# Block sums of a 7-product down projection: made on GpSimd in earlier stages and passed through DRAM, instead of inside the projection

## The chip, the cores and the metric

One core of one Trainium2 chip. The metric is the device time of one execution in microseconds, as the median of several runs.

## The reference, cut to what matters

One decoder layer on x of 1024 rows and 1024 columns, all in float32:

```python
p = rms_norm(x, norm_mix) @ w_in              # one projection into three groups of heads
y = concat(conv_mixer(p), nsa_mixer(p), rwkv7(p))
x = x + y @ w_out                             # out-projection, residual
h = rms_norm(x, norm_ffn)
g = causal_dwconv(h @ w_gate, width 3)        # 2816 channels
x = x + (silu(g) * (h @ w_up)) @ w_down       # w_down is 2816 x 1024
return rms_norm(x, norm_final)
```

The change concerns the last product, A @ W with A = silu(g) * (h @ w_up).

## The kernel before, in words

A tile framework puts the instructions of the whole program in an order for each engine ahead of time; every engine then runs its own list strictly in that order, and waits where an operand is not there. Every DMA is issued by SP, which also works through its list in order and waits there for the data that a store needs or for the buffer that a load fills. Float32 products are made of three TensorE matmuls: `split` (L118 to L121) lets ACT round an operand to a high part and DVE subtract it to get the low part, and `mm3` (L226 to L229) adds high x high, low x high and high x low.

The stages, by the time of the profiled execution:

- To about 400 us: norm, in-projection, convolution and most of the RWKV part. The RWKV part has two halves of channels and two of the sequence; for each there is a solve (`V`, L513 to L534: a chain of dependent small operations on GpSimd, each L528 product followed by an L530 sum) and then a chain of matmuls on TensorE (`C`, first the 32x32 matmuls of L550, which read the tile `DF`). The solve V10 and the solve V11, and the chains C10 and C11, run beside the attention, with high priority. The solve writes its result to DRAM; `DF` is loaded from there (L543).
- 400 to about 717 us: the attention, eight query tiles `attn_tile` (L821 to L933) in the order 7, 6, 5, 4, 0, 3, 2, 1. Of each tile, two operations are made on GpSimd (L849, L857: the sums of the compressed scores, whose result goes to the transposes L862 on TensorE) and most of the softmax on DVE (L911 scales the probabilities `pp`). The tile's result goes to DRAM as `md` (L933). SP loads a tile's queries `QS` (L831, L832) when the buffer of two tiles earlier is free.
- To about 850 us: the out-projection (`out_tile`, L959 on) reads `md` back, splits it (`mix`), multiplies with w_out, and adds the residual; then the second norm and the operands of h for the gate and up products.
- 850 to 1264 us: `ffn_up`. For each of 22 blocks of 128 channels it makes gate and up of all 1024 rows with 7 products instead of 8 (Winograd's form of Strassen's scheme on 2x2 blocks), 84 matmuls per block. GpSimd makes four sums `S` of the block's weights per product group (L1050), about one block ahead. DVE makes the block of A in two tiles `prod` of 128 channels by 512 rows (L1079), which are stored to DRAM (`pd`).
- 1264 to 1531 us: `ffn_down`, the same scheme on A @ W: A is cut into 2x2 blocks (two halves of channels, 11 blocks of 128 each, by two halves of rows), W into 2x2 blocks (two halves of channels by two halves of columns). Seven runs, each one product of 11 f-steps x 4 row tiles x 3 matmuls, 924 matmuls of 128x512 in all. Run 1 needs A11 and B11 as they are; the others need the sums S1 to S4 of blocks of A and T1 to T4 of blocks of W. The helpers g1 to g3 (L1123 to L1169) load 55 blocks of A and 55 of W of 256 KB and make these sums in place, per f-step, in the run that needs them first: T3 and T4 on DVE, the other six on GpSimd, 88 in all (all recorded as L1124). Each run then splits both operands (tiles `sp`). Besides, GpSimd adds the residual (L1202, 16 times) and multiplies by the norm's weight (8 times).

Of the kernel before, what the change touches and what calls it, by code (L numbers as in the profile page):

```python
# [19 lines left out]
class K:  # L20
    def __init__(self, tc, a, out, ctx, bufs=None):
        self.tc, self.nc, self.a, self.out, self.ctx = tc, tc.nc, a, out, ctx
        self.B = dict(b2=20, wraw=2, whi=2, wlo=2, t4=4, rraw=2, cy=2, hx=12, ev=3, cv=2, lora=2, rb=20, at=2, pr=7, rt=2,
                      QS=2, pp=6, q8=2, pT=5, xn=8, h2=14, graw=2, prod=4, ft=4, u=4, wr2=4, wfh=3, wfl=3, S=2, p1=2, om=6, grow=2, pre=2, ap=(), wf=("own", "wf", "om"), hd=("vector",) * 4, tq=((0, 1, 2, 3),), ttag=("tr", "rw"),
# [999 lines left out]
    def ffn_up(self, H):  # L1024
        nc, a = self.nc, self.a
        v, s, gp = nc.vector, nc.scalar, nc.gpsimd
        self.pd = [[self.dram.tile([P, 512], F32, name=f"pd{ft}{h}") for h in range(2)] for ft in range(22)]
        for ft in range(22):
# [7 lines left out]
            def prod(bank, raw, part, first=False):  # L1036
                w = self.B["wf"][(self.nw if ft >= self.B["pre"] else self.nw % 2) % len(self.B["wf"])]
# [64 lines left out]
            out(0, u2)  # L1102

    def ffn_down(self):
# [9 lines left out]
        def A(t, m, k, f):

            nc.sync.dma_start(t, self.pd[k * F + f][1 - m])
            return t

        def Bw(t, k, n, f):
            nc.sync.dma_start(t, W[(k * F + f) * P:(k * F + f) * P + P, n * 512:n * 512 + 512])  # L1120
            return t

        def e(key, x, y, z, op=ALU.subtract):  # L1123
            getattr(nc, self.B["de"][key]).tensor_tensor(x, y, z, op=op)  # L1124
            return x
        a11, a21, b11, b12, b22 = ([None] * F for _ in range(5))
# [4 lines left out]
        def g1(f):  # L1131
            a11[f] = A(self.b2() if f < 10 else x4("r4"), 0, 0, f)
            b11[f] = Bw(self.b2() if f < 10 else x4("r4"), 0, 0, f)
            return a11[f], b11[f]
# [8 lines left out]
        def g2(f):  # L1143
            e("T1", b11[f], b12[f], b11[f])
            e("T2", b12[f], b22[f], b11[f])
            return A(x4("ta"), 0, 1, f), Bw(x4("tb"), 1, 0, f)

        def g4(f):
            t = Bw(x4("tb"), 1, 0, f)
            e("T4", t, t, b12[f])  # L1150
            a22 = A(x4("ta"), 1, 1, f)
            e("S1", a21[f], a21[f], a22, ALU.add)
            e("S2", a11[f], a22, a11[f])
            return a22, t

        def g6(f):
            return a11[f], b12[f]

        def g6b(f):
            e("S4", a11[f], A(x4("ta"), 0, 1, f), a11[f])  # L1160

        def g5(f):
            return a21[f], b11[f]

        def g3(f):
            return a11[f], b22[f]
# [236 lines left out]
```

## Time and profile before

| | us |
|---|---|
| three runs | 1527.68, 1532.06, 1541.17; median 1532.06 |
| the profiled execution | 1533.06, of which the span that the trace shows is 1531.3 |
| TensorE busy | 1431.6 (93%) |
| TensorE's weight loads | 1135.8 (74%) |
| VectorE (DVE) | 1042.6 (68%) |
| ScalarE (ACT) | 684.2 (45%) |
| GpSimd (POOL) | 488.6 (32%) |

The span is cut below into the stages named above. A row of a stage gives the busy time of each engine in it, the share of full speed at which TensorE's clock was granted, and the share of time and the rate at which DMAs moved data.

### The profile page before, as it was taken

To read this page: it belongs to the slowest core of one execution; us is meant where nothing else is said; L and a number is where in the kernel's file an instruction comes from. 1 tells how busy PE (TensorE), PEld (TensorE's weight loads), DVE (VectorE), ACT (ScalarE), POOL (GpSimd) and SP (SyncE) were. 2 spreads that over 40 slices of the span, in tenths; PEclk is the share of its full clock that TensorE was granted. 3 is DMA by queue.
4 is the path that set the end of the run, shared out by engine and by line. 5 is a ranking of instruction groups with operands and counts; after the bars stand their busy time and mean duration, and the time that the engine had idled before them with its cause. 6 is when DMAs were issued, how large, how long until landed. Compare 5 with 4: busy or idle time off the path is not lost.

```text
span 1531.3 us, 22605 instructions
## 1 busy us (share of the span) xinstructions
PE 1431.6 (93%) x8025; PEld 1135.8 (74%) x8025; DVE 1042.6 (68%) x2193; ACT 684.2 (45%) x1361; POOL 488.6 (32%) x585
## 2 busy tenths in 40 slices
PE   6999679999799999998899999999999999897897
PEld 5887457777677777775687788888888887685686
DVE  6247695453586778587267767767767668979976
ACT  6432354534266567677133534334433333343453
POOL 1004887910420050001001223323323315849820
PEclk9999787989799999999999999999999999998999
DMA  6142223433710112114522122222222229163302
GB/s 188 37 120 56 52 83 87 144 93 108 193 32 15 32 39 64 55 39 129 179 90 76 55 69 83 89 77 83 77 89 83 67 93 375 43 203 121 117 1 110
DMA packets 182916, 143.41 MB, mean 94 GB/s; under 512 B 53715, under 2 KB 143124, under 8 KB 182804
## 3 DMA queue, kind: packets, MB, share of 16 engines
q1 hardware_dynamic: 182804, 141.98, 30.5%
q8 instruction: 63, 1.03, 0.3%
q14 instruction: 49, 0.40, 0.1%
HBM read 103.92 MB, written 38.01 MB: 93 GB/s over the span
## 4 chain that ended last, share of the span: by engine, by line
PE 75%; DVE 11%; DMA 5%; POOL 3%; issue 2%; ACT 1%; SPq 1%; DVEq 0%; POOLq 0%; ACTq 0%
PE mm L229 13%; PE gb L229 12%; PE ga L229 9%; PE rw L229 8%; PE gc L229 8%; PE tr L918 5%; PE av L926 4%; DVE sp L121 4%; PE tr L229 3%; PE mm L893 2%; PE mm L894 2%; POOL sT L530 1%; POOL sx L528 1%; PE pm L493 1%; DVE cacc L272 1%
## 5 line engine op out<-in xcount | busy, mean ns | idle before, releaser
L229 PE MATMUL mm<-hT,whi 128*128 128x512 f32 x608 | 204.8, 418 | 0.0
L229 PE MATMUL mm<-hT,wlo 128*128 128x512 f32 x304 | 127.8, 422 | 20.3 <-DVE wlo L121 20.3
L229 PEld LDWEIGHTS mm<-hT,whi 128*128 128x128 f32 x608 | 120.2, 200 | 29.4 <-issue 1.6
L1050 POOL TENSOR_TENSOR S<-wraw,wr 128x512 f32<-128x512 f32 x22 | 28.5, 1297 | 257.9 <-DVE or L107 96.1
L921 ACT ACTIVATE pT<-tr 128x512 f32<-128x512 f32 (+1 forms) x152 | 80.0, 537 | 62.6 <-PE tr L918 61.3
L926 PE MATMUL av<-pT,V 128*64 128x128 f32 x1056 | 95.2, 286 | 4.0 <-ACT pT L921 3.9
L279 POOL TENSOR_TENSOR cacc<-cacc,ctap 128x512 f32<-128x512 f32 x60 | 91.1, 1542 | 17.7 <-ACT ctap L278 17.5
L229 PE MATMUL rw<-sp,sp 128*128 128x512 f32 x330 | 90.0, 397 | 7.1 <-DVE sp L121 6.6
L918 PE MATMUL tr<-idn,pp 128*128 128x128 f32 x528 | 89.6, 288 | 0.1
L229 PEld LDWEIGHTS mm<-hT,wlo 128*128 128x128 f32 x304 | 60.8, 200 | 38.6 <-DVE wlo L121 21.4
L229 PE MATMUL tr<-sp,sp 128*128 128x512 f32 x330 | 88.4, 395 | 0.0
L229 PE MATMUL rw<-woh,mix 128*128 128x512 f32 x240 | 78.9, 405 | 6.4 <-DVE xn L976 5.2
L926 PEld LDWEIGHTS av<-pT,V 128*64 128x64 f32 x1056 | 59.2, 136 | 28.9 <-issue 11.0
L229 PEld LDWEIGHTS rw<-sp,sp 128*128 128x128 f32 x330 | 62.6, 191 | 22.6 <-DVE sp L121 8.8
L893 PE MATMUL mm<-KH,QS 128*128 128x512 f32 (+2 forms) x192 | 74.1, 394 | 4.0 <-DMA QS<-qd 2.5
L918 PEld LDWEIGHTS tr<-idn,pp 128*128 128x128 f32 x528 | 55.7, 141 | 28.6 <-issue 27.3
L121 DVE TENSOR_TENSOR sp<-b,sp 128x512 fp32r<-128x512 f32 x60 | 65.5, 1104 | 13.4 <-ACT sp L120 13.3
L229 PEld LDWEIGHTS tr<-sp,sp 128*128 128x128 f32 x330 | 63.1, 191 | 13.4
L849 POOL TENSOR_TENSOR cmp<-cmp,cmx 128x512 f32<-128x512 f32 (+7 forms) x8 | 5.4, 680 | 206.2 <-DVE cmx L847 137.0
L120 ACT ACTIVATE whi<-wraw 128x512 fp32r<-128x512 f32 x55 | 34.6, 628 | 78.7 <-PE mm L229 60.3
L121 DVE TENSOR_TENSOR wlo<-wraw,whi 128x512 fp32r<-128x512 f32 x55 | 42.3, 771 | 34.9 <-ACT whi L120 34.8
L528 POOL TENSOR_TENSOR sx<-sN,sT 128x60 f32<-128x60 f32 (+24 forms) x124 | 43.8, 353 | 65.4 <-DMA sN<-dn 57.0
(460 smaller groups left out, 3846.3 us busy)
## 6 DMA issues: line engine op xcount, KB each, us to landing
wr<-in_ffn_w_gate_dram SPq DMA_DIRECT2D x44, 256.0 KB
wraw<-in_ffn_w_up_dram SPq DMA_DIRECT2D x44, 256.0 KB
pd<-prod SPq DMA_DIRECT2D x44, 256.0 KB
ta<-pd SPq DMA_DIRECT2D x33, 256.0 KB
wraw<-in_w_in_dram SPq DMA_DIRECT2D x30, 256.0 KB
tb<-in_ffn_w_down_dram SPq DMA_DIRECT2D x22, 256.0 KB
rb<-in_ffn_w_down_dram SPq DMA_DIRECT2D x20, 256.0 KB
qd<-ev SPq DMA_DIRECT2D x16, 256.0 KB
```

Source lines behind the costliest of these rows:

```text
L120: self.nc.scalar.activation(hi, src, AF.Copy)
L121: getattr(self.nc, eng).tensor_tensor(lo, src, hi.bitcast(F32), op=ALU.subtract)
L229: mm = lambda l, r, **k: self.nc.tensor.matmul(out, l, r, skip_group_check=more, **k)
L272: nc.vector.scalar_tensor_tensor(t, y[:, d:d + T], w, t, op0=ALU.mult, op1=ALU.add)
L279: nc.gpsimd.tensor_tensor(t[:, o:o + 512], t[:, o:o + 512], z, op=ALU.add)
L528: v_.tensor_tensor(x, N[:, q, q + 1:32].unsqueeze(2).to_broadcast([P, n, w]), Tm[:, q, 0:w].unsqueeze(1).to_broadcast([P, n, w]), op=ALU.mult)
L893: pe.matmul(pts[g][:, 0:n], QS[:, r, g, :], KH[g][hf][:, ks], start=True, stop=False)
L894: pe.matmul(pts[g][:, 0:n], QS[:, r, g, :], KL[g][hf][:, ks], start=False, stop=True)
L918: pe.transpose(pt[:, o:o + P], Ps[g][:, kt * P:kt * P + P], self.idn)
L921: s.activation(pT[:, 0:n], pt[:, 0:n], AF.Copy)
L926: pe.matmul(av[g * 64:g * 64 + 64, r * P:r * P + P], self.V[kk // 2][:, kk % 2, vo + g * 64:vo + g * 64 + 64], pT[:, o:o + P], start=first ...
L1050: gp.tensor_tensor(t, x, y, op=op)
```

## The change

Each of the eight sums of blocks is made once, in an earlier stage, by GpSimd, and stored to DRAM. `down_sums(f)` loads the four blocks of W of one f-step, makes T1 to T4 in place with four GpSimd operations (L945 to L948) in the rotating tiles `wraw`, `whi`, `wlo` (six buffers of 256 KB), and stores them; it is called for two f-steps behind each of the first five query tiles and for one behind the sixth. `ffn_up` visits the channel blocks in the order 0, 11, 1, 12, ..., so that behind each odd one all four blocks of A of an f-step are there; GpSimd makes S1 to S4 of them (L1131 to L1134), and seven blocks instead of four are stored per pair. `ffn_down` loads two finished operands per f-step and run, 154 blocks, and makes no sums. The loads in all: 44 more of W in the attention, 44 more (154 for 110) in the down projection; the stores: 44 more in the attention, 33 more (77 for 44) in `ffn_up`.

```diff
...
+ds=((0, 1), (2, 3), (4, 5), (6, 7), (8, 9), (10,), (), ()), prod=5
...
+    def down_sums(self, f):
+        nc, W = self.nc, self.a["ffn_w_down"][0]
+        b = {}
+        for k, n in ((0, 0), (0, 1), (1, 1), (1, 0)):
+            t = b[k, n] = self.wt([P, 512], ("wraw", "whi", "wlo")[self.nd % 3])
+            self.nd += 1
+            nc.sync.dma_start(t, W[(k * 11 + f) * P:(k * 11 + f) * P + P, n * 512:n * 512 + 512])
+        tt = nc.gpsimd.tensor_tensor
+        tt(b[0, 0], b[0, 1], b[0, 0], op=ALU.subtract)
+        tt(b[0, 1], b[1, 1], b[0, 1], op=ALU.subtract)
+        tt(b[1, 1], b[1, 1], b[0, 0], op=ALU.subtract)
+        tt(b[1, 0], b[1, 0], b[1, 1], op=ALU.subtract)
+        for n, t in (("T1", b[0, 0]), ("T3", b[0, 1]), ("T2", b[1, 1]), ("T4", b[1, 0])):
+            self.td[n, f] = d = self.dram.tile([P, 512], F32, name=f"td{n}{f}")
+            self.st.dma_start(d, t)
...
-        for ft in range(22):
+        for nft, ft in enumerate(f for i in range(11) for f in (i, i + 11)):
...
-                self.st.dma_start(self.pd[ft][half], p)
+                pp[1 - half, nft % 2] = p
+                if (half, nft % 2) != (0, 0):
+                    store(f"A{2 - half}{nft % 2 + 1}", ft % 11, p)
...
+            if nft % 2:
+                f = ft % 11
+                s1, s2, s4 = (self.xt([P, 512], "prod") for _ in range(3))
+                gp.tensor_tensor(s1, pp[1, 0], pp[1, 1], op=ALU.add)
+                gp.tensor_tensor(pp[1, 0], pp[0, 0], pp[1, 0], op=ALU.subtract)
+                gp.tensor_tensor(s2, pp[1, 1], pp[1, 0], op=ALU.subtract)
+                gp.tensor_tensor(s4, pp[0, 1], s2, op=ALU.subtract)
+                for n, t in (("S1", s1), ("S3", pp[1, 0]), ("S2", s2), ("S4", s4)):
+                    store(n, f, t)
...
-        def g7(f):
-            a21[f] = A(x4("r4"), 1, 0, f)
-            b12[f] = Bw(self.rb(), 0, 1, f)
-            b22[f] = Bw(self.rb() if f < 9 else x4("r4"), 1, 1, f)
-            e("S3", a11[f], a11[f], a21[f])
-            return a11[f], e("T3", x4("tb"), b22[f], b12[f])
...
+        def parts(pa, pb, home):
+            def get(f):
+                ta, tb = self.b2(), home()
+                nc.sync.dma_start(ta, self.pd[pa, f])
+                if pb[0] == "T":
+                    nc.sync.dma_start(tb, self.td[pb, f])
+                else:
+                    k, n = int(pb[1]) - 1, int(pb[2]) - 1
+                    nc.sync.dma_start(tb, W[(k * F + f) * P:(k * F + f) * P + P, n * 512:n * 512 + 512])
+                return ta, tb
+            return get
...
-        run(Y, g7, True, LL, d7)
-        run(X, g2, False, LL, d2)
+        run(Y, "S3", "T3", True, LL, d7)
+        run(X, "A12", "B21", False, LL, d2)
...
...
         for n, i in enumerate(order):
             self.attn_tile(i)
+            for f in self.B["ds"][n]:
+                self.down_sums(f)
```

How the change moves instructions is read from the order in which each engine has them (a name behind an arrow is read, one ahead of it written).

GpSimd in the solve V10, beside query tile 7. Before (L528 and L530 are the solve, in turn):

```order
L528 TENSOR_TENSOR sx<-sN,sT 128x30
L530 TENSOR_TENSOR sT<-sT,sx 128x30
L528 TENSOR_TENSOR sx<-sN,sT 128x29
L530 TENSOR_TENSOR sT<-sT,sx 128x29
L528 TENSOR_TENSOR sx<-sN,sT 128x28
L530 TENSOR_TENSOR sT<-sT,sx 128x28
L528 TENSOR_TENSOR sx<-sN,sT 128x54
L530 TENSOR_TENSOR sT<-sT,sx 128x27x2
L528 TENSOR_TENSOR sx<-sN,sT 128x52
L530 TENSOR_TENSOR sT<-sT,sx 128x26x2
```

With the change, from the same place on:

```order
L528 TENSOR_TENSOR sx<-sN,sT 128x28
L945 TENSOR_TENSOR wraw_5086<-whi_5088,wraw_5086 128x512
L530 TENSOR_TENSOR sT<-sT,sx 128x28
L946 TENSOR_TENSOR whi_5088<-wlo_5090,whi_5088 128x512
L528 TENSOR_TENSOR sx<-sN,sT 128x54
L849 TENSOR_TENSOR cmp_4552<-cmp_4552,cmx_4554 128x512
L947 TENSOR_TENSOR wlo_5090<-wlo_5090,wraw_5086 128x512
L945 TENSOR_TENSOR whi_5106<-wlo_5108,whi_5106 128x512
L530 TENSOR_TENSOR sT<-sT,sx 128x27x2
L948 TENSOR_TENSOR wraw_5092<-wraw_5092,wlo_5090 128x512
L528 TENSOR_TENSOR sx<-sN,sT 128x52
L857 TENSOR_TENSOR cmp_4552<-cmp_4552,csm_4558 128x512
```

All 44 sums of W (11 f-steps of L945 to L948) stand between the first and the last operation of this one solve, and also the two L849 and L857 of query tiles 7 and 6; behind the solve there is none. On SP the 44 loads and 44 stores stand in one piece too, among them the loads of `QS` of tiles 6 and 5 and the store of `md` of tile 7, and behind them the stores of the solve's result and the load of `DF`. On TensorE the first L550 of C10 stands, before, in the middle of tile 6, and with the change right behind the first scores of tile 5; the transposes L862 of tile 6 stand 44 rows ahead of it.

TensorE where the attention passes into the out-projection (`av` L926 and `tr` L918 are the attention; L631 and L636 the last matmuls of the RWKV part, whose result is multiplied in as a gate and stored to `md`; L229 with `woh`, `wol` and `mix` the out-projection). Before:

```order
L918 MATMUL tr_7448<-idn,pp_7422 128x128 x2
L631 MATMUL rw_4437<-idn,gyc_4414 128x128 x4
L636 MATMUL rw_4445<-lora_772,lw_w 128x512
L893 MATMUL mm_7668<-KH_4523,QS_7495 128x256
L894 MATMUL mm_7668<-KL_4529,QS_7495 128x256
L926 MATMUL av_7190<-pT_7442,V_4537 64x128 x4
L918 MATMUL tr_7472<-idn,pp_7457 128x128 x4
```

and further on, in the same tail, matmuls of the out-projection among those of the last attention tile:

```order
L926 MATMUL av_7505<-pT_7595,V_4537 64x128 x4
L926 MATMUL av_7505<-pT_7623,V_4537 64x128 x4
L862 MATMUL tr_7629<-idn,cmp_7506 32x128 x4
L918 MATMUL tr_7654<-idn,pp_7639 128x128 x4
L229 MATMUL rw_7914<-woh_7754,mix_7900 128x512
L229 MATMUL rw_7914<-wol_7755,mix_7900 128x512
L229 MATMUL rw_7942<-woh_7760,mix_7900 128x512
L229 MATMUL rw_7942<-wol_7761,mix_7900 128x512
```

With the change:

```order
L918 MATMUL tr_7930<-idn,pp_7915 128x128 x4
L926 MATMUL av_7725<-pT_7907,V_4537 64x128 x4
L918 MATMUL tr_7958<-idn,pp_7943 128x128 x4
L926 MATMUL av_7725<-pT_7935,V_4537 64x128 x4
L926 MATMUL av_7725<-pT_7963,V_4537 64x128 x4
L631 MATMUL rw_4437<-idn,gyc_4414 128x128 x4
L636 MATMUL rw_4445<-lora_772,lw_w 128x512
L229 MATMUL rw_8134<-woh_7974,mix_8120 128x512
L229 MATMUL rw_8134<-wol_7975,mix_8120 128x512
```

L631 and L636 have moved behind the attention's last matmul, straight ahead of the out-projection's first one, and none of the out-projection's matmuls stands among those of the attention any more.

GpSimd in `ffn_up`. Before (L1050 makes the sums `S` of weights, L1065 fills two columns of the gate's input):

```order
L1050 TENSOR_TENSOR S_9602<-wr_2028_9575,wr_2029_9576 128x512
L1050 TENSOR_TENSOR S_9604<-S_9602,wraw_9573 128x512
L1065 MEMSET graw_9610 128x2
L1050 TENSOR_TENSOR S_9606<-wraw_9573,wr_2028_9575 128x512
L1050 TENSOR_TENSOR S_9608<-wraw_9574,S_9604 128x512
L1050 TENSOR_TENSOR S_9760<-wr_2061_9733,wr_2062_9734 128x512
L1050 TENSOR_TENSOR S_9762<-S_9760,wraw_9731 128x512
L1065 MEMSET graw_9768 128x2
```

With the change (the same lines are L1072 and L1087 there):

```order
L1072 TENSOR_TENSOR S_10684<-wr_2249_10657,wr_2250_10658 128x512
L1072 TENSOR_TENSOR S_10686<-S_10684,wraw_10655 128x512
L1087 MEMSET graw_10692 128x2
L1131 TENSOR_TENSOR prod_10487<-prod_10327,prod_10484 128x512
L1132 TENSOR_TENSOR prod_10327<-prod_10307,prod_10327 128x512
L1133 TENSOR_TENSOR prod_10488<-prod_10484,prod_10327 128x512
L1134 TENSOR_TENSOR prod_10489<-prod_10464,prod_10488 128x512
L1072 TENSOR_TENSOR S_10688<-wraw_10655,wr_2249_10657 128x512
L1072 TENSOR_TENSOR S_10690<-wraw_10656,S_10686 128x512
```

The four sums of A of a pair of blocks stand in one piece between the second and the third `S` of the block after the next.

## Rows read from the trace of the kernel before

**Rows 1.** Stages: stretch, length, busy PE, PEld, DVE, ACT, POOL (count), PEclk, DMA share, GB/s.
```profile
400.00:700.00 300.00, 293.75 (x2639) 221.81 (x2639) 225.48 (x842) 193.66 (x440) 50.56 (x141) 0.99 0.18 47
850.00:1264.00 414.00, 409.05 (x1796) 333.57 (x1795) 281.71 (x389) 162.63 (x262) 120.95 (x106) 1.00 0.26 80
1264.00:1523.00 259.00, 234.51 (x962) 186.71 (x960) 219.96 (x264) 107.44 (x200) 147.59 (x90) 0.95 0.40 135
```
**Rows 2.** The same for tiles `sp` alone, without a column for POOL.
```profile
1264.00:1523.00 259.00, 226.54 (x924) 179.94 (x924) 162.87 (x152) 87.87 (x152) 0.95 0.40 135
1470.00:1510.00 40.00, 40.00 (x179) 33.09 (x178) 19.34 (x30) 15.06 (x26) 1.00 0.14 52
```
**Rows 3.** Waits, down projection: who waits <- for whom: us in all, times, longest.
```profile
PE ga L229 <- DVE sp L121: 16.5, 11, 3.3
PE rw L229 <- DVE sp L121: 6.6, 4, 3.2
```
**Rows 4.** Groups of DVE: busy us, mean ns | idle before; first 1263 to 1470, then 1470 to 1520.
```profile
L121 DVE TENSOR_TENSOR sp<-b,sp 128x512 fp32r<-128x512 f32 x47 | 56.5, 1220 | 6.9 <-ACT sp L120 6.8
...
L121 DVE TENSOR_TENSOR sp<-b,sp 128x512 fp32r<-128x512 f32 x13 | 8.9, 686 | 4.6 <-ACT sp L120 4.6
```
**Rows 5.** Groups of POOL in the down projection.
```profile
L1124 POOL TENSOR_TENSOR b<-ta,b 128x512 f32<-128x512 f32 x20 | 33.9, 1694 | 6.9 <-DVE sp L121 6.9
...
L1202 POOL TENSOR_TENSOR y<-y,wraw 128x512 f32<-128x512 f32 x16 | 26.5, 1660 | 11.4 <-DVE y L1213 9.7 <-DMA wraw<-xd 1.1 <-DVE sp L121 0.6
```
**Rows 6.** The window in the down projection in which DMAs moved most.
```profile
1270.00:1290.00 20.00, 16.82 (x74) 13.63 (x73) 19.62 (x21) 6.62 (x12) 13.79 (x9) 0.99 1.04 379
```
**Rows 7.** Groups of POOL, 1020 to 1080, in the gate and up stage.
```profile
L1050 POOL TENSOR_TENSOR S<-wraw,wr 128x512 f32<-128x512 f32 x3 | 3.9, 1298 | 24.5 <-DVE wlo L121 11.6 <-DVE om L121 11.6 <-DVE wfl L121 1.3
```
**Rows 8.** Timeline of POOL: start, us, operation [idle before <- releaser].
```profile
1074.32 1.30 POOL L1050 TENSOR_TENSOR S<-wraw,wr 128x512 f32<-128x512 f32 x1 [11.56 <-DVE om L121]
```
**Rows 9.** Timeline of DVE in that gap: the product that the channel sums read.
```profile
1064.26 0.68 DVE L1079 TENSOR_TENSOR prod<-u,ft 128x512 f32<-128x512 f32 x1
```
**Rows 10.** Timeline of POOL: first and last operation of the solve V10, and a sum between.
```profile
407.50 0.24 POOL L528 TENSOR_TENSOR sx<-sN,sT 128x31 f32<-128x31 f32 x1 [14.74 <-DMA sN<-dn]
...
412.55 1.04 POOL L849 TENSOR_TENSOR cmp<-cmp,cmx 128x512 f32<-128x512 f32 x1
...
433.18 0.33 POOL L530 TENSOR_TENSOR sT<-sT,sx 128x8 f32<-128x8 f32 x1
```
**Rows 11.** Timeline of SP: the load of DF.
```profile
440.10 0.34 SPq L543 DMA_DIRECT2D DF<-dt  x1
```
**Rows 12.** L550 to 560 us: count, ns min/median/max, first and last start.
```profile
L550 PE MATMUL rw<-DF,GA x32: 191/191/212, 474.0 to 475.0; 32*32 32x32 f32 x32
```
**Rows 13.** Timeline of PE: the first scores of query tile 5.
```profile
510.59 0.42 PE L893 MATMUL mm<-KH,QS 128*128 128x384 f32 x1
```
**Rows 14.** Stretch 412 to 510: all engines, then line L911 alone (DVE's busy time).
```profile
412.00:510.00 98.00, 96.41 (x893) 71.45 (x891) 73.01 (x255) 63.48 (x127) 20.50 (x55) 1.00 0.11 25
...
412.00:510.00 98.00, 18.84 (x30) 1.00 0.11 25
```
**Rows 15.** Groups of DVE: L911 beside the solve (412 to 433), then without (445 to 475).
```profile
L911 DVE TENSOR_SCALAR pp<-pp,sm 128x640 f32<-128x640 f32 x8 | 4.6, 613 | 0.0
...
L911 DVE TENSOR_SCALAR pp<-pp,sm 128x640 f32<-128x640 f32 x4 | 2.0, 551 | 0.0
```
**Rows 16.** Stretch 700 to 745: the passage from the attention to the out-projection.
```profile
700.00:745.00 45.00, 34.95 (x235) 25.04 (x234) 21.48 (x72) 23.43 (x58) 3.98 (x4) 0.95 0.53 156
```
**Rows 17.** Timelines there: PE's av, ACT's split of mix, PE's out-projection.
```profile
716.48 0.66 PE L926 MATMUL av<-pT,V 128*64 128x128 f32 x8 [1.14 <-ACT pT L921]
...
741.45 0.63 ACT L120 ACTIVATE mix<-mix 128x512 fp32r<-128x512 f32 x1 [4.58 <-DMA mix<-md]
...
743.79 0.79 PE L229 MATMUL rw<-woh,mix 128*128 128x512 f32 x1 [5.18 <-DVE xn L976]
```

More of the change, by code (lines that the diff above doesn't have):

```diff
@@ L1026, in ffn_up, with store @@
         v, s, gp = nc.vector, nc.scalar, nc.gpsimd
-        self.pd = [[self.dram.tile([P, 512], F32, name=f"pd{ft}{h}") for h in range(2)] for ft in range(22)]
-        for ft in range(22):
+        self.pd = {(n, f): self.dram.tile([P, 512], F32, name=f"pd{n}{f}") for f in range(11) for n in ("A11", "A12", "A22", "S1", "S2", "S3", "S4")}
+        pp = {}
+        def store(n, f, t):
+            self.st.dma_start(self.pd[n, f], t)
+        for nft, ft in enumerate(f for i in range(11) for f in (i, i + 11)):
             c = slice(ft * P, ft * P + P)
@@ L1036, in prod @@
             def prod(bank, raw, part, first=False):
[L1037 removed]
+                w = self.B["wf"][(self.nw if nft >= self.B["pre"] else self.nw % 2) % len(self.B["wf"])]
                 self.nw += 1
@@ L1086, in ffn_up @@
             add(u2, Bk, p1)
-            if ft >= self.B["pre"]:
+            if nft >= self.B["pre"]:
                 prod(C, S1, H["T1"], True)
@@ L1091, in ffn_up @@
             add(u3, Bk, p1)
-            if ft >= self.B["pre"]:
+            if nft >= self.B["pre"]:
                 prod(A, up2, H["B21"])
@@ L1110, in ffn_down @@
         fs = range(F)
-        x4 = lambda tag: self._t(self.x4, [P, 512], F32, tag, None)
         wt = lambda tag: self.wt([P, 512], tag)
[L1114 to L1126, printed above, removed]
         gf = [wt("wlo") for _ in range(2)]
@@ L1129, in ffn_down, with run @@
             nc.sync.dma_start(gf[d], a["norm_final"][d * 512:d * 512 + 512].rearrange("(o d) -> o d", o=1).to_broadcast([P, 512]))
[L1131 to L1134, printed above, removed]
-        def g7(f):
-            a21[f] = A(x4("r4"), 1, 0, f)
-            b12[f] = Bw(self.rb(), 0, 1, f)
-            b22[f] = Bw(self.rb() if f < 9 else x4("r4"), 1, 1, f)
-            e("S3", a11[f], a11[f], a21[f])
-            return a11[f], e("T3", x4("tb"), b22[f], b12[f])
[L1143 to L1166, printed above, removed]
+        def parts(pa, pb, home):
[9 more added lines that the diff above has]
+            return get
         h2 = lambda: self._t(self.xo, [P, 512], F32R, "h2", "sp")
-        def run(banks, get, first, late, done, after=None, lt=h2):
+        def run(banks, pa, pb, first, late, done, lt=h2):
+            get = parts(pa, pb, self.rb if lt is h2 else self.b2)
             pend = []
@@ L1179, in run @@
                 self.split(q[2], q[3], pb)
-                if after:
-                    after(f)
                 if f < F - late:
@@ L1262, in ffn_down @@
         x4r = lambda tag: self._t(self.x, [P, 512], F32, tag, None)
-        run(X, g1, True, LL, d1)
-        run(Y, g7, True, LL, d7)
-        run(X, g2, False, LL, d2)
-        run(Y, g4, False, LL, d4)
+        run(X, "A11", "B11", True, LL, d1)
+        run(Y, "S3", "T3", True, LL, d7)
+        run(X, "A12", "B21", False, LL, d2)
+        run(Y, "A22", "T4", False, LL, d4)
         Z = [self.bank(t) for t in ("rw", "rw", "tr", "tr")]
-        run(Z, g6, True, LL, d6, g6b)
-        run(Z, g5, False, LL, d5)
-        run(Z, g3, False, L, d3, lt=lambda: self.rb(dt=F32R, name="sp"))
+        run(Z, "S2", "T2", True, LL, d6)
+        run(Z, "S1", "T1", False, LL, d5)
+        run(Z, "S4", "B22", False, L, d3, lt=lambda: self.rb(dt=F32R, name="sp"))
     def build(self):
@@ L1330, in build @@
         self.attn_load()
-        for i in order:
+        self.nd, self.td = 0, {}
+        for n, i in enumerate(order):
             self.attn_tile(i)
+            for f in self.B["ds"][n]:
+                self.down_sums(f)
         self.wout_load()
```

4 lines of the change are left out of this document (2 added, 2 removed).

## The prediction, on record before the changed kernel ran

> **What bounds the kernel now.** I read the stages first, then the waits of the last one, then the engines that the change loads. The stages [rows 1] show TensorE busy for 294 of 300 us in the attention and 409 of 414 us in the gate and up stage: what is added there to another engine is free until TensorE has to wait for it. The down projection is different: 234.5 of 259 us busy, and the busy time itself is stretched. Its 924 matmuls took 226.5 us, but in the quiet last part, with GpSimd idle, 179 of them took 40 us [rows 2], 0.223 us each; 924 x 0.223 = 206 us, and all 962 of the stage 215 us. So 259 - 215 = 44 us lie there in waits and in a clock at 0.95. The waits name the place: TensorE waits for the low part `sp` of an operand, 16.5 + 6.6 us in the two largest groups [rows 3]. The DVE groups say why: beside the block sums a split took 1220 ns, without them 686 ns [rows 4]. GpSimd's block sums took 1694 ns each [rows 5], and a split must wait for some of them.
>
> **The down projection.** 88 sums go, from GpSimd and DVE alike. What is left per f-step and run is two loads, two ACT copies, two subtractions on DVE and 12 matmuls, 2.68 us of TensorE. DVE needs 2 x 0.69 = 1.4 us (2.4 us at the contended 1220 ns, beside the 24 GpSimd operations that stay, 16 of them at 1660 ns [rows 5]), so it keeps up either way. The loads: 154 + 16 blocks of 256 KB are 44.6 MB; at 379 GB/s [rows 6] 118 us of 215, and 512 KB per f-step 1.4 us of 2.68. SP issues about 170 loads; at 0.34 us each, as for the load of `DF` [rows 11], that is 58 us. So TensorE should run nearly at its own rate. Of the 44 us I leave 6: some 3 us for the start, as in the first 20 us shown, where TensorE was busy for 16.8 [rows 6], and 3 us for the seven handovers of runs with GpSimd's residual adds. **-38 us** (bounds -20, if DMA or the adds make half the waits again, to -44).
>
> **Gate and up stage.** 44 sums on GpSimd, four per pair of channel blocks. A sum of this size took 1298 ns [rows 7], so 5.2 us per pair. GpSimd sat idle for 11.6 us ahead of one weight sum, till 1074.3 [rows 8], and the product that the sums read was made at 1064.3 [rows 9]: they fit into that gap. In the order they stand between the second and the third S of the block after next, which GpSimd makes about one block ahead. In some pairs they stand among four S in a row, and the DVE meets 5 us more of GpSimd per pair. DVE has 282 of 414 us of work [rows 1]. 33 more stores of 256 KB at a quarter of the DMA time are hidden. **+2 us** (0 to +8).
>
> **Attention.** The call list would spread the sums of W over six query tiles; the order has put all 44 into the single solve V10. That solve lasted from 407.5 to 433.5 us in small dependent operations [rows 10]. A 512-wide sum inside it took 1.04 us [rows 10], in the down projection up to 1.69 [rows 5]: 44 of them are 46 to 74 us, and the solve becomes 72 to 100 us long. The buffers also pace it: six for blocks of four, so a block row waits for the stores of the row ahead and for loads into the freed buffers; by the same durations and about 6 us for a store and a load (an estimate: the SP load of DF was issued 7 us behind the solve [rows 10, 11], store in between), two rows take some 16 us, 11 rows about 88 us. The solve then ends at 495 to 507 and `DF` is there about 10 us later (before, it was loaded at 440.1 and first used at 474.0, some 30 us of slack [rows 11, 12]). TensorE now reaches L550 behind the first scores of tile 5, which started at 510.6 [rows 13], plus whatever tiles 7 and 6 lose. So the wait there is 0 to 6 us. The other cost is DVE. L911, 30 times and 18.8 us between 412 and 510 [rows 14], took 613 ns beside the solve's small operations and 551 ns without [rows 15]. If a 1.04 to 1.69 us sum holds it up by a third of its length, that is 0.4 to 0.5 us each, 12 to 16 us; DVE has 25 of 98 us free there [rows 14], so most is absorbed. C10's matmuls, which filled TensorE's gaps in tile 6, now come later. **+8 us** (0 to +20).
>
> This is where a rule speaks against the change. The Trainium skill, "SBUF — State Buffer", section "Who interferes with whom", says that GpSimd shares one pair of SBUF ports with DVE under an exclusive lock: a DVE instruction with two SBUF inputs contends with a GpSimd instruction that reads SBUF, and a tensor_scalar in a two-port mode is blocked for the whole of it. The split agrees (1220 against 686 ns [rows 4]). By the rule the lock does not go with the change but moves into the attention, and an L911 there that always meets a sum at its start would lose 1.04 to 1.69 us; that is the third case below.
>
> **Handover to the out-projection.** The solve delays C10 and with it V11 and C11: L631 and L636 now stand behind the attention's last matmul, ahead of the first of the out-projection. TensorE lost 10 of 45 us there already [rows 16], 5.2 us of it in one wait [rows 17]. With L636 last, the gate's product (DVE), its store as `md`, its load, the split and then the first matmul follow each other: before, ACT waited 4.6 us for the load of `mix` and split it in 0.63 us, and the matmul came 1.7 us later [rows 17]; with a store of about the same length ahead, some 12 to 14 us without anything to fill them, against about 5. **+8 us** (0 to +14). The w_out loads, behind the burst on SP, are 200 us early and cost nothing.
>
> **Sum** against the profiled execution of 1533.1 us, 1 us above the median shown: 1533 - 38 + 2 + 8 + 8 = **1513 us**.
>
> **Rivals.**
> - *Attention and handover cost nothing.* The burst ends before L550, L911 is absorbed, and the scheduler's other work fills the passage. For it: the 30 us of slack before. Then 1533 - 38 + 2 = 1497.
> - *The lock sets the attention's pace.* 30 L911 at 1.0 us more are 30 us on a DVE with 25 us free, and the two-input operations suffer too: 12 us more than in my sum, 1525. Against it: L911 beside the small operations lost only 62 ns [rows 15].
> - *Slower: the burst overruns.* GpSimd and SP are in order, so a store of T that waits for GpSimd holds the next loads, and the solve waits for them. If a block row takes 13 us and not 8, the burst ends at 407 + 143 = 550, `DF` is there at 560, and TensorE, in order, stands at L862 of tile 6 and at L550 for some 43 us. Then 1533 - 38 + 2 + 43 + 8 = 1548. It decides from about 10.5 us per row (solve till 523, wait 15 us); the forecast is lost against the time before at 12 us per row, where the wait is 28 us. Against it: by the rows, 8 us.
> - *The down projection does not reach TensorE's rate.* Twice the loads in flight and an SP list that waits for buffers bring half the waits back: -20, so 1531; with half of that, 1525. For it: DMAs were saturated for 20 us at its start [rows 6].
> - *The change does not do what it says*: the sums of W are not spread over six tiles. That is so by the order, and in the sum.
>
> **Chances.** Forecast 0.47 (own range 1502 to 1524), nothing lost 0.17, lock 0.14, overrun 0.12, down projection slow 0.10. About 1% is what a measurement can tell, so faster means below 1516.7 and slower above 1547.4. Faster: three fifths of the forecast (0.29), all of the second, and a little of the last ones, 0.49. Slower: most of the overrun, 0.11. The rest, 0.40, within. Leaving out a third of the second case and two thirds of the overrun (0.13) gives 1494 to 1546.
>
> **What would show it.** In the down projection: a stage of about 220 us, splits at 0.7 us, no large group in which TensorE waits for DVE `sp`; if such waits stay, or DMA takes their place, the first step is wrong. In the attention: L945 to L948 from 410 to about 500, a wait of TensorE at L550 or L862 (none, a few, or tens of us tells the first three apart), the mean of L911 there, and the length of 400 to 700. At the passage: the gap between the last `av` and the first matmul with `woh`. In the gate and up stage: TensorE's waits, and whether the S of the block after come late. The prediction fails if the time from 400 to 850 grows by more than 30 us, or the down projection stays above 240.

## The result

The changed kernel took 1516.7 us (median of four runs, 1514.5 to 1519.3) against 1533.3 us of the kernel before; the ratio is 0.989, 95% interval 0.984 to 0.994. The forecast of 1513 us was 4 us low and its sign right. The profiled execution took 1516.7 us, its span 1515.0.

The stages of the changed kernel, with the columns of [rows 1]:

```profile
400.00:700.00 300.00, 287.04 (x2514) 214.41 (x2515) 225.22 (x789) 185.26 (x419) 107.87 (x185) 0.97 0.40 118
850.00:1264.00 414.00, 402.80 (x1772) 326.62 (x1771) 300.88 (x413) 163.91 (x273) 174.21 (x142) 1.00 0.29 93
1264.00:1515.00 251.00, 241.50 (x1063) 199.20 (x1061) 163.48 (x281) 116.32 (x216) 50.07 (x34) 0.99 0.62 210
```

The last of them for tiles `sp` alone, as in [rows 2]:

```profile
1264.00:1515.00 251.00, 210.26 (x924) 173.47 (x924) 119.57 (x154) 88.21 (x154) 0.99 0.62 210
```

The 924 matmuls of the down projection take 210 us, not 226.5. GpSimd has 34 operations left in the window, where it had 90. The attention has the GpSimd time instead (108 us for 51), and TensorE is 6.7 us less busy there. Between 1304 and 1324 us DMAs moved data without a pause, and TensorE was busy all the time (columns as in [rows 1]):

```profile
1304.00:1324.00 20.00, 20.00 (x90) 16.58 (x89) 11.98 (x15) 7.85 (x14) 5.87 (x4) 1.00 1.05 388
```

Fixed windows don't follow the stages when these shift. So I use three marks that each kernel's trace has: the start of the first matmul `ga` with `wfl` (start of the gate and up stage; a few of its matmuls with `whi` stand ahead of it), the start of the last `gb` with `om` (its end), and the end of the span. All kernels of this study, in us:

| kernel | median | start of gate and up | to its end | down projection |
|---|---|---|---|---|
| before, in four series | 1529.2 to 1533.5 | 829.6 | 446.1 | 255.6 |
| the change | 1516.7 | 850.2 | 448.3 | 216.5 |
| 1 channel sums moved alone | 1506.6 | 827.8 | 447.7 | 227.3 |
| 2 weight sums moved alone | 1530.4 | 846.9 | 446.3 | 234.7 |
| 3 weight sums spread over the tiles | 1513.5 | 857.6 | 444.1 | 216.5 |
| 4 unused sums in the down projection, GpSimd | 1565.0 | 864.6 | 448.5 | 255.7 |
| 5 before, all sums on DVE | 1500.4 | 829.6 | 445.2 | 225.9 |
| 6 as 1, sums of W on DVE | 1504.5 | 835.2 | 448.5 | 225.4 |
| 7 transfers of W alone | 1494.9 | 830.3 | 448.2 | 216.5 |
| 8 sums in the attention alone | 1518.0 | 853.1 | 448.3 | 216.5 |
| 9 as 4, all on DVE | 1533.4 | 852.1 | 448.3 | 231.2 |
| 10 the change, sums of W on DVE | 1531.0 | 864.1 | 448.3 | 217.1 |
| 11 as 5, no GpSimd in the down projection | 1498.1 | 829.4 | 446.4 | 218.3 |
| 12 as 6, no GpSimd in the down projection | 1505.5 | 831.3 | 448.5 | 223.3 |

The three spans of a line are one profiled execution's; its time is up to 7 us from the median. The last one repeats: 216.5 us in each of the four kernels that share the change's down projection (the change, 3, 7, 8), 217.1 in the tenth. The first one scatters: among kernels that add no sums to the attention from 827.8 to 835.2, and kernels 4 and 9, whose orders up to the down projection are that of the change, gave 864.6 and 852.1 for its 850.2. Of kernel 4's 14.4 us, 12.0 are busy time of the same 5193 matmuls, at a mean granted clock of 0.92 for 0.94.

5193 matmuls stand ahead of the first mark in the kernel before and in the change. Here is TensorE up to that mark in three stretches (length, busy, clock, DMA share, GB/s), first before, then with the change:

```profile
0.00:400.00 400.00, 358.64 (x1938) 0.90 0.37 103
400.00:700.00 300.00, 293.75 (x2639) 0.99 0.18 47
700.00:829.60 129.60, 119.55 (x620) 0.97 0.41 130
...
0.00:400.00 400.00, 354.63 (x1947) 0.91 0.38 105
400.00:700.00 300.00, 287.04 (x2514) 0.97 0.40 118
700.00:850.20 150.20, 132.39 (x734) 0.94 0.38 120
```

So of the 20.6 us, 18.5 are idle time: 4.0 before 400 us, 6.7 from there to 700 us, 7.8 behind it. The other 2.1 us are busy time. The 4.0 us are not shown to be the change's: kernels without sums in the attention sit idle for 40.9 (kernel 12) to 45.1 us (kernel 5) before 400 us, the change for 45.4.

In the changed kernel one wait of TensorE for `sp` is left; this group had 16.5 us and 11 waits in [rows 3]:

```profile
PE ga L229 <- DVE sp L121: 0.5, 1, 0.5
```

The splits are faster than in [rows 4], though not as fast as in a stretch without GpSimd, since its 24 adds and multiplications are still there (DVE, 1287 to 1470):

```profile
L121 DVE TENSOR_TENSOR sp<-b,sp 128x512 fp32r<-128x512 f32 x74 | 59.4, 809 | 3.1 <-ACT sp L120 2.9
L121 DVE TENSOR_TENSOR sp<-rb,sp 128x512 fp32r<-128x512 f32 x65 | 56.4, 868 | 49.7 <-ACT sp L120 49.7
```

In the attention, GpSimd's timeline has the first sum in the solve V10, and the solve's last operation:

```profile
407.26 1.29 POOL L945 TENSOR_TENSOR wraw<-whi,wraw 128x512 f32<-128x512 f32 x1 [0.39 <-DVE mx L897]
...
503.11 0.46 POOL L530 TENSOR_TENSOR sT<-sT,sx 128x8 f32<-128x8 f32 x1
```

TensorE's summary of L550, with the first start in C10 and the last in C11:

```profile
L550 PE MATMUL rw<-DF,GA x64: 190/192/212, 514.9 to 655.4; 32*32 32x32 f32 x64
```

The solve ends 70 us later than in [rows 10]; 11 block rows in 96 us are 8.8 us each. TensorE did not wait for `DF` there. What it waited for between 400 and 850 was this, the two largest groups, and the same two in the kernel before:

```profile
PE rw L229 <- ACT mix L120: 17.0, 3, 13.3
PE mm L893 <- DVE mx L897: 7.7, 7, 2.5
...
PE rw L229 <- ACT mix L120: 1.3, 1, 1.3
PE mm L893 <- DVE mx L897: 1.3, 2, 1.0
```

The 13.3 us are the passage to the out-projection, in PE's timeline:

```profile
731.35 0.66 PE L926 MATMUL av<-pT,V 128*64 128x128 f32 x8 [0.16 <-ACT pT L921]
...
732.52 1.12 PE L636 MATMUL rw<-lora,lw_w 64*128 64x512 f32 x2
746.97 0.80 PE L229 MATMUL rw<-woh,mix 128*128 128x512 f32 x1 [13.32 <-ACT mix L120]
```

in DVE's, where the gate's product `gz` is made:

```profile
734.73 0.69 DVE L637 TENSOR_TENSOR gz<-gz,rw 128x512 f32<-128x512 f32 x1
```

in SP's:

```profile
732.74 0.37 SPq L933 DMA_DIRECT2D md<-mix  x1
...
736.02 0.43 SPq L638 DMA_DIRECT2D md<-gz  x1
...
741.14 0.43 SPq L984 DMA_DIRECT2D mix<-md  x1
```

and in ACT's:

```profile
746.29 0.63 ACT L120 ACTIVATE mix<-mix 128x512 fp32r<-128x512 f32 x1 [1.76 <-DMA mix<-md]
```

The store at 732.7 is that of the last query tile, which the first tile of the out-projection does not read. It reads the gate's product, stored at 736.0; its load is issued at 741.1. Between the two, SP issues seven loads of w_out, of x and of `grow`, back to back but for some half a microsecond. So these loads hold the load of `md` for up to 4.6 us; whether its data would have come earlier without them no run shows.

After the wait the clock is low for a while: the first matmuls of the out-projection start 0.43 us apart, at the lower of the two levels (1.2 GHz), and from about 751.4 on 0.23 us apart. The stretch 740 to 760, columns as in [rows 1], has a mean of 0.72:

```profile
740.00:760.00 20.00, 11.87 (x42) 9.31 (x43) 4.68 (x7) 3.78 (x6) 0.56 (x1) 0.72 1.07 336
```

### The profile page after: what moved, and what is told of

Same layout as the page of the kernel before. It is cut to its first block, busy times and chain, and to the rows that moved or that the text cites. A ratio compares the mean times of both kernels' runs of the same rounds, so it can differ in the third digit from the quotient of the medians.

```text
span 1515.0 us, 22973 instructions
## 1 busy us (share of the span) xinstructions
PE 1418.2 (94%) x8025; PEld 1128.7 (75%) x8025; DVE 1001.0 (66%) x2171; ACT 684.0 (45%) x1361; POOL 500.2 (33%) x607
## 4 chain that ended last, share of the span: by engine, by line
PE 78%; DVE 10%; DMA 4%; POOL 2%; issue 2%; ACT 2%; SPq 1%; DVEq 0%; ACTq 0%; POOLq 0%
PE mm L229 13%; PE gb L229 12%; PE rw L229 10%; PE ga L229 8%; PE gc L229 8%; PE tr L229 5%; PE tr L918 4%; PE av L926 4%; PE mm L893 2%; PE mm L894 2%; POOL sx L528 1%; PE rw L493 1%; POOL sT L530 1%; DVE pp L897 1%; DVE pp L911 1%
## 5 line engine op out<-in xcount | busy, mean ns | idle before, releaser
L229 PE MATMUL mm<-hT,whi 128*128 128x512 f32 x608 | 201.6, 413 | 0.0
L229 PE MATMUL mm<-hT,wlo 128*128 128x512 f32 x304 | 126.1, 416 | 18.8 <-DVE wlo L121 18.8
L229 PEld LDWEIGHTS mm<-hT,whi 128*128 128x128 f32 x608 | 118.3, 197 | 28.5 <-issue 1.4
L926 PE MATMUL av<-pT,V 128*64 128x128 f32 x1056 | 96.4, 289 | 1.3 <-ACT pT L921 1.1
L229 PE MATMUL rw<-woh,mix 128*128 128x512 f32 x240 | 79.4, 406 | 17.0 <-ACT mix L120 17.0
L918 PE MATMUL tr<-idn,pp 128*128 128x128 f32 x528 | 91.6, 292 | 0.5 <-DVE pp L911 0.3
L121 DVE TENSOR_TENSOR sp<-rb,sp 128x512 fp32r<-128x512 f32 x66 | 57.1, 865 | 50.4 <-ACT sp L120 50.3
L1072 POOL TENSOR_TENSOR S<-wraw,wr 128x512 f32<-128x512 f32 x22 | 28.5, 1295 | 181.0 <-DVE or L107 79.2
L229 PEld LDWEIGHTS mm<-hT,wlo 128*128 128x128 f32 x304 | 59.9, 197 | 37.0 <-DVE wlo L121 20.1
L893 PE MATMUL mm<-KH,QS 128*128 128x512 f32 (+2 forms) x192 | 77.3, 407 | 10.0 <-DVE mx L897 7.7
L229 PE MATMUL rw<-sp,sp 128*128 128x512 f32 x330 | 86.1, 389 | 0.0
L229 PE MATMUL tr<-sp,sp 128*128 128x512 f32 x330 | 85.9, 389 | 0.0
L926 PEld LDWEIGHTS av<-pT,V 128*64 128x64 f32 x1056 | 59.9, 138 | 27.3 <-issue 13.0
L528 POOL TENSOR_TENSOR sx<-sN,sT 128x60 f32<-128x60 f32 (+24 forms) x124 | 47.4, 382 | 97.4 <-DMA sN<-dn 90.5
L918 PEld LDWEIGHTS tr<-idn,pp 128*128 128x128 f32 x528 | 56.5, 142 | 30.0 <-issue 27.9
L120 ACT ACTIVATE sp<-rb 128x512 fp32r<-128x512 f32 x66 | 41.6, 630 | 74.0 <-PE tr L229 37.5
L121 DVE TENSOR_TENSOR sp<-b,sp 128x512 fp32r<-128x512 f32 x88 | 68.8, 789 | 5.3 <-ACT sp L120 5.1
L229 PEld LDWEIGHTS rw<-sp,sp 128*128 128x128 f32 x330 | 62.0, 188 | 12.8
L229 PEld LDWEIGHTS tr<-sp,sp 128*128 128x128 f32 x330 | 62.0, 188 | 12.8
L904 ACT ACTIVATE pp<-pp,nm 128x640 f32<-128x640 f32 (+3 forms) x64 | 57.6, 904 | 23.7 <-DVE nm L902 22.1
```

The lines of the kernel that those rows point to most:

```text
L120: self.nc.scalar.activation(hi, src, AF.Copy)
L121: getattr(self.nc, eng).tensor_tensor(lo, src, hi.bitcast(F32), op=ALU.subtract)
L229: mm = lambda l, r, **k: self.nc.tensor.matmul(out, l, r, skip_group_check=more, **k)
L528: v_.tensor_tensor(x, N[:, q, q + 1:32].unsqueeze(2).to_broadcast([P, n, w]), Tm[:, q, 0:w].unsqueeze(1).to_broadcast([P, n, w]), op=ALU.mult)
L893: pe.matmul(pts[g][:, 0:n], QS[:, r, g, :], KH[g][hf][:, ks], start=True, stop=False)
L904: s.activation(Ps[g], Ps[g], AF.Exp, bias=nm[:, g:g + 1], scale=-1.0, accum_out=sm[:, g:g + 1])
```

## The experiments

**1 and 2. Each half alone.** The first kernel calls no `down_sums` and makes T1 to T4 in `ffn_down` as before; the second leaves `ffn_up` as before and makes S1 to S4 in `ffn_down`.

```diff
-ds=((0, 1), (2, 3), (4, 5), (6, 7), (8, 9), (10,), (), ())
+ds=((), (), (), (), (), (), (), ())
...
+            return A(x4("ta"), "S3", f), e("T3", x4("tb"), b22[f], b12[f])
```

> The channel sums S1 to S4 in the gate and up stage and through DRAM as in the change; the sums T1 to T4 of the weights stay inside the down projection as before, nothing is added to the attention. Theory 1 (the attention's and the passage's loss of 23 us comes from the 44 sums of W alone, the gain of 40 us is shared by both halves): 400 to 850 us as before, gate and up stage +3 us, down projection 267 to about 247 us: about 1516 us. Rival (the gain comes only when all sums are gone, since a split waits for the last of them): down projection above 258 us, time 1527 or more.

> The sums of W in the attention and through DRAM as in the change; the channel blocks as before (made in the order 0 to 21, their sums inside the down projection). Theory 1: the attention and the passage lose the same 23 us, the gate and up stage nothing, the down projection gains about 20 of 40 us: about 1536 us, no better than before. Rival (the W sums were the ones that held up the splits): down projection below 235 us, about 1522 us.

The buffers of the down projection (`r4`, `ta`, `tb`) are divided anew in both, to fit. Ratios to before 0.983 (0.980 to 0.987) and 0.999 (0.997 to 1.001). For the first, theory 1 had given 1516 us and a stage of 247; it came to 1506.6 and 227.3. For the second it gave the stage's 20 us rightly. The attention pays for the weights alone (846.9 against 827.8). In the down projection the first half gives 28.3 us and the second 20.9, together more than the 39.1 of both: the halves are not two separate sums of waits, they ease the same thing. Moving the weights cost what it brought; without it the change would have been 8 to 10 us faster (by the ratios, whose intervals overlap a little, and by the medians).

**3. The weight sums spread.**

```diff
+        self.tok = self.small([P, 1], "tok")
+        nc.gpsimd.tensor_copy(self.tok, mf[:, 0:1])
...
+            if (k, n) == (0, 0):
+                nc.gpsimd.tensor_copy(t[:, 0:1], self.tok)
             nc.sync.dma_start(t, W[(k * 11 + f) * P:...
```

> The change, with the first weight block of each f-step made to wait for the result of its query tile (a one-column copy on GpSimd from that result into the block's buffer ahead of its load), so that the 44 sums are spread over the tiles and the solve V10 stands without them, L631 ahead of the attention's end and out-projection matmuls among its last ones, as before. Theory 1 (it is the packing into the solve that costs: late C10 and C11, an empty passage): of the 23 us some 5 remain, about 1499 us. Rival (44 sums and 88 DMAs cost DVE and the queues the same wherever they stand in the attention): 1512 us or more.

0.988 (0.985 to 0.992), no different from the change's 0.989 by the intervals. V10 is short again (it ends at 432) and out-projection matmuls run inside the attention's tail, from 742.4, but the last `av` starts at 764.8 instead of 731.7. The loss did not go with the packing: theory 1 falls on that point.

**4. Sums that nobody reads.**

```diff
                 self.split(q[2], q[3], pb)
+                for eng in dummy:
+                    getattr(nc, eng).tensor_tensor(x4("ta"), pa, pb, op=ALU.subtract)
...
+        run(Y, "S3", "T3", True, LL, d7, dummy=("gpsimd", "vector"))
...
```

> The change, and in the down projection the same 66 GpSimd and 22 DVE operations of 128x512 per run and f-step as before, on the finished operands, with results that nobody reads. Theory A (the 40 us were waits of a split for a block sum): the splits are slow again, some 1200 ns, but the stage grows by 8 us at most, to 236: about 1525 us. Theory B (they were the shared access of DVE and GpSimd, whoever waits for whom): the stage goes back above 250 us, 1540 us.

The 66 and 22 sums are those of the whole stage. 1565.0 us (1.021, 1.017 to 1.025), and the down projection at 255.7 us, to 0.1 us that of the kernel before. (Theory B's 1540 us for the whole was too low: this execution lost 14.4 us more than the change ahead of the stage.) No split waits for a sum there, yet TensorE's waits for `sp`, DVE's splits and GpSimd's sums are nearly those of before. Waits of PE:

```profile
PE rw L229 <- DVE sp L121: 17.5, 15, 2.7
PE ga L229 <- DVE sp L121: 7.9, 8, 2.7
```

Groups of DVE, 1300 to 1568:

```profile
L121 DVE TENSOR_TENSOR sp<-b,sp 128x512 fp32r<-128x512 f32 x87 | 97.5, 1129 | 3.4 <-ACT sp L120 3.3
L121 DVE TENSOR_TENSOR sp<-rb,sp 128x512 fp32r<-128x512 f32 x66 | 80.9, 1226 | 9.7 <-ACT sp L120 9.7
```

These means mix two kinds of splits. The shortest, median and longest of the second group, in ns:

```profile
L121 DVE TENSOR_TENSOR sp<-rb,sp x66: 677/1238/1787, 1301.8 to 1524.2; 128x512 fp32r<-128x512 f32 x66
```

Of the 153 splits between 1300 and 1560 us, 81 took 0.6 to 0.8 us and 65 took 1.6 to 1.8 us; the 62 beside which GpSimd had no operation took 686 ns on the mean. Groups of POOL, the whole stretch:

```profile
L1179 POOL TENSOR_TENSOR ta<-b,rb 128x512 f32<-128x512 f32 x66 | 110.9, 1703 | 42.7 <-DMA rb<-tdT 25.3 <-DVE ta L1179 9.3 <-DMA b<-pdS 7.4
```

Theory B holds as far as it says that the two engines slow each other; that it is an access which they share is not shown by this. One thing is open, the operands that these sums hold longer; the ninth run is for that.

**5, 6, 11 and 12. GpSimd out of the down projection.** The fifth kernel is that of before with `de=dict(S3="vector", T1="vector", ...)`, all eight on DVE (T3 and T4 were there already, so 66 of the 88 sums move); the eleventh also has

```diff
-            nc.gpsimd.tensor_tensor(t, t, x, op=ALU.add)
+            v.tensor_tensor(t, t, x, op=ALU.add)
...
-            nc.gpsimd.tensor_tensor(y1[tt], y1[tt], gf[0], op=ALU.mult)
+            v.tensor_tensor(y1[tt], y1[tt], gf[0], op=ALU.mult)
```

and the same for `s4`. The sixth and twelfth do the same to the first.

> The kernel before, with the six block sums that GpSimd makes in the down projection given to DVE: all 88 sums on DVE, no other stage touched. Theory B (the shared access of DVE and GpSimd made the 40 us): splits and sums at about 0.69 us; DVE is then late only in the fourth run (3 sums and 2 splits, 3.45 us, against 2.68 us of matmuls, some 9 us in 11 f-steps); down projection, from the last gate and up matmul on, 255.6 to about 228 us, 1505 us. Theory A (a split waits for a sum, whoever makes it; now 66 more sums stand ahead of splits on DVE itself): 250 us or more, 1525 or more.

> The channel sums alone moved as in the change, and the four sums of W that stay in the down projection made by DVE (T1 and T2 taken from GpSimd). Theory B: down projection 227 to about 219 us, close to the 216.5 of the change, with no cost in the attention: about 1499 us. Theory A: 22 more sums on DVE delay the splits, 230 us or more, 1510.

> The fifth experiment, with the 16 residual adds and 8 multiplications of the down projection on DVE too, so that GpSimd does nothing there. Theory B and what was left (one wait of 4.4 us and a fall of the clock beside the residual adds): down projection 225.9 to about 221 us, 1496 us. Rival (DVE, busy for 200 of 240 us there, becomes the bound with 24 x 0.69 = 16.6 us more): 228 us or more, 1503 or more.

> The sixth experiment (channel sums moved as in the change, sums of W inside the down projection on DVE), with the residual adds and multiplications on DVE too: no GpSimd in the down projection and no weight sums in the attention. Theory B: splits at 0.69 us, DVE some 170 of 217 us; down projection about 218 us, gate and up stage +2, about 1495 us, the best of all. Rival (the start of the second run, which waited for 4.2 us for an operand, is the rest): 224 us, 1502.

Ratios 0.979 (0.975 to 0.983), 0.981 (0.977 to 0.985), 0.974 (0.969 to 0.979), 0.980 (0.974 to 0.985). The eleventh has the lowest time of those that do all of the work, 1498.1 us (1494.6 to 1501.5; the fifth's 1500.4 is within the noise of it), and has the old data flow: 88 sums in place, no additional transfer. Its DVE has 112 more operations than the change's in this stage, and every split takes the quiet time. Groups of DVE, 1290 to 1500:

```profile
L121 DVE TENSOR_TENSOR sp<-b,sp 128x512 fp32r<-128x512 f32 x47 | 32.0, 689 | 5.7 <-ACT sp L120 5.7
L1124 DVE TENSOR_TENSOR b<-ta,b 128x512 f32<-128x512 f32 x20 | 13.7, 689 | 0.0
```

All of TensorE's waits for `sp`:

```profile
PE ga L229 <- DVE sp L121: 1.4, 1, 1.4
PE rw L229 <- DVE sp L121: 0.3, 1, 0.3
```

Taking only the block sums off GpSimd gives 29.7 us (the fifth), taking its 24 other operations off too gives 37.3 (the eleventh). The change, which leaves these 24 on GpSimd, gains 39.1. So all but 1.8 us of its gain can be had with the sums still made inside the stage. In the twelfth the rival was right (223.3 us), and the sixth lies between its two theories: in both TensorE waited at the start of the second run, 4.2 and 4.1 us. There ACT waited for a store of S (waits of ACT in the twelfth, 1290 to 1330):

```profile
ACT y L1235 <- DMA pdS<-prod: 8.4, 2, 7.0
```

GpSimd's timeline shows why the store was late:

```profile
1296.18 19.13 POOL L1131 TENSOR_TENSOR prod<-prod,prod 128x512 f32<-128x512 f32 x1 [37.96 <-DVE prod L1101]
1315.39 1.29 POOL L1132 TENSOR_TENSOR prod<-prod,prod 128x512 f32<-128x512 f32 x1
```

as it does in the sixth:

```profile
1300.04 19.13 POOL L1131 TENSOR_TENSOR prod<-prod,prod 128x512 f32<-128x512 f32 x1 [37.90 <-DVE prod L1101]
```

The window of that stretch in the twelfth shows that DVE was busy for 18.2 of 19 us in the meantime:

```profile
1296.00:1315.00 19.00, 18.72 (x83) 15.16 (x82) 18.16 (x31) 7.39 (x13) 18.82 (x1) 1.00 0.52 190
```

**7, 8 and 10. What costs the attention.** In the seventh the four lines of `tt(...)` are gone; the eighth keeps them on four fixed buffers without `dma_start`; the tenth has `tt = nc.vector.tensor_tensor`.

> The change without the 44 GpSimd sums in the attention (left out: T1 to T4; the blocks of W are loaded and stored as they are). Theory lock (GpSimd's sums cost the attention its 23 us): 5 us of them stay, attention to up 432 us, about 1499 us. Rival (88 transfers of 256 KB between 400 and 500 and the list of SP cost it): 445 us or more, 1512 or more.

> The change with the 44 GpSimd sums in the attention on four buffers that are filled once with zeros, without their 44 loads and 44 stores; the down projection loads blocks of W in place of T1 to T4 (left out: the sums of W). Some 20 of the sums stand ahead of the solve V10, the others in it. Theory lock: the loss stays, 445 us or more from the attention to the gate and up stage, 1511 or more. Rival (transfers): 432 us, about 1499 us.

> The change, with the 44 sums of W in the attention on DVE instead of GpSimd. 44 x 0.69 = 30 us more on DVE, which is busy for 225 of 300 us there. Theory lock (a sum on GpSimd holds DVE up and stretches the solve): attention to up about 437 us, down projection 216.5, about 1501 us. Rival (any 44 sums of 512 columns beside the softmax make TensorE late, and the passage stays empty since L631 stands late in this order too): 445 us or more, 1511 or more.

The seventh kernel leaves out the sums of W, the eighth stores none of them and uses blocks of W in their place; both results are for time alone. The transfers cost nothing (0.975, 0.972 to 0.979; up starts at 830.3, with 264 GB/s between 400 and 500). But without the sums TensorE has its old order back as well: the first matmul with `woh` starts at 718.8 and the last `av` at 736.6, as before (719.4 and 735.6). So the seventh does not tell the sums' own time from the order that they lead to.

The sums without the transfers bring a loss of the same size (0.991, 0.988 to 0.994; up starts at 853.1), but not the same loss. At the passage TensorE waits 5.8 us for `mix`, not 17.0, and its longest wait stands ahead of the attention:

```profile
PE rw L474 <- DVE cum L472: 10.5, 1, 10.5
```

DVE's sums cost more still (0.996, 0.993 to 0.999; the median is 14 us above the change's with the same down projection), though L911 is not slowed there. Its first mark is 13.9 us behind the change's: 3.2 us are idle time of TensorE, the rest is busy time of the same number of matmuls. The groups of L911 between 412 and 510, in the kernel before:

```profile
L911 DVE TENSOR_SCALAR pp<-pp,sm 128x640 f32<-128x640 f32 x16 | 9.3, 625 | 0.1
L911 DVE TENSOR_SCALAR pp<-pp,sm 128x1024 f32<-128x1024 f32 x8 | 5.7, 749 | 0.1
```

in the seventh:

```profile
L911 DVE TENSOR_SCALAR pp<-pp,sm 128x640 f32<-128x640 f32 x16 | 9.2, 613 | 0.1
L911 DVE TENSOR_SCALAR pp<-pp,sm 128x1024 f32<-128x1024 f32 x8 | 5.8, 770 | 0.1
```

in the change:

```profile
L911 DVE TENSOR_SCALAR pp<-pp,sm 128x640 f32<-128x640 f32 x16 | 12.0, 791 | 0.1
L911 DVE TENSOR_SCALAR pp<-pp,sm 128x1024 f32<-128x1024 f32 x8 | 8.9, 1151 | 0.1
```

and in the tenth:

```profile
L911 DVE TENSOR_SCALAR pp<-pp,sm 128x640 f32<-128x640 f32 x16 | 9.0, 596 | 0.1
L911 DVE TENSOR_SCALAR pp<-pp,sm 128x1024 f32<-128x1024 f32 x8 | 5.7, 749 | 0.1
```

The loss of the tenth has other parts: an empty passage again, and DVE in order behind transfers of W. Its largest waits of PE at the passage, and of DVE behind such a load:

```profile
PE rw L229 <- ACT mix L120: 17.0, 3, 12.7
...
DVE wraw L945 <- DMA whi<-in_ffn_w_down_dram: 5.4, 1, 5.4
```

So a GpSimd beside DVE is not needed for a loss of this size. The third comes nearest to sums without an empty passage, and there TensorE's idle time up to the first mark is 71.8 us, for 57.7 before and 76.1 in the change, with 13.9 us more of busy time than before. No kernel here has the sums in the attention together with a full passage and no late DVE; what share of the 20 us each of these has is open.

**9. The fourth with DVE.** All `dummy` entries are `"vector"`.

> The fourth experiment again, with all 88 unused sums of the down projection on DVE instead of 66 of them on GpSimd: the same operations, the same operands held as long, no GpSimd beside the splits. Theory B (shared access): the stage returns from 255.7 to about 222 us, 1530 us in all, as the packed attention of this kernel costs what it costs. Rival (operands held by the unused sums, or DVE's and GpSimd's time as such, made the 39 us): 245 us or more, 1550 or more.

The stage falls from 255.7 to 231.2 us with the same operands held: at least 24.5 of the 39.2 us that the unused sums cost came from GpSimd making them. The other 14.7 are 9 more than theory B allowed. TensorE's waits for splits:

```profile
PE ga L229 <- DVE sp L121: 5.1, 3, 2.7
PE rw L229 <- DVE sp L121: 5.0, 2, 4.5
```

DVE has up to five operations per f-step in the fourth run now, 3.4 us at 686 ns each, for 2.68 us of matmuls. Whether the operands that are held have a part in the 14.7 us is not shown. Total 1533.4 us, 0.998 (0.995 to 1.001).

## Why the prediction was right, step by step

- **Down projection, -38 us:** -39.1 between the marks. The size was right. Of the reason, half: the step named both the sums' length beside the splits and that "a split must wait for some of them". The unused sums (4) bring the whole time back without that dependence; the sums on DVE (11) keep the dependence and end 1.8 us behind the change. So the dependence counts for little here, and what GpSimd and DVE cost each other for nearly all.
- **Gate and up stage, +2 us:** +2.2. TensorE's waits there hardly grew, the 44 sums sat in GpSimd's gaps. The other kernels with the same work took 447.7 to 448.5 us, only the third 444.1.
- **Attention, +8, and passage, +8:** 20.6 us to the start of the gate and up stage, where the sum had 16. TensorE's idle time grew by 6.7 us between 400 and 700 and by 7.8 us behind that, near both terms; the 4.0 us before 400 and the 2.1 us of busy time were in no term. The row of 8 us came out at 8.8, the solve's end (495 to 507) at 503.6, the wait at L550 (0 to 6) at nothing. L911 lost 7.0 us in all between 412 and 510 (16 x 166, 8 x 402 and 6 x 195 ns over before), not 12 to 16; TensorE waited 7.7 us for the first maximum `mx` of DVE, 6.4 more than before.
- **The step that failed in it:** "the w_out loads, behind the burst on SP, are 200 us early and cost nothing". Their last load was issued at 743.3, before at 712.2; six of the loads of w_out are issued between 734.0 and 740.0, and four of them stand between the store of `gz` and the load of `md`. The wait at the passage was forecast at 12 to 14 us and took 13.3, but that is luck in part: the prediction gave the store 4.6 us, and the 5.1 us that passed between store and load were filled by these loads and three others. And the lower clock behind the wait was not in the sum.
- **Rivals:** "nothing lost" did not happen. The burst did not overrun: 8.8 us per row, where that case begins at 10.5. The down projection reached TensorE's rate though DMAs were saturated. (In that rival, "half of that" is 1513 + 9 = 1522, not 1525; nothing rests on it.) Of the lock as the attention's pace there is a part, 7 us, 0.23 us for an L911 on the mean. The rule that I weighed (the Trainium skill, "SBUF — State Buffer", section "Who interferes with whom") agrees with the down projection: most splits took 1.6 to 1.8 us beside unused GpSimd sums, and 686 ns without. In the attention it doesn't price the loss, since the tenth kernel lost as much without GpSimd's sums.

## What to carry to other kernels

When an engine's operations get slow in a stretch, ask first what runs beside them, and try to give the neighbour's work to the slow engine itself: 66 sums and 24 other operations more on DVE made DVE's stage 37 us shorter here, and no data had to move. Test a wait for a result by making that result unused; if the time stays, the wait was only the label. And an operation that is moved into a dense stage is paid for in that stage's order: see which instructions it pushes behind the stage's end, and what its loads push back on an in-order queue.
